# A hybrid layer on one core: one store for four normalisers, Silu in place of Sigmoid and multiply, and VectorE's work moved at five spots

## The chip, the cores and the metric

The kernel runs on one core of a Trainium2 chip, in one launch. The metric is the device time of one execution in microseconds (us). "Before" was run three times, and one more execution was profiled.

## The reference

One layer of a decoder trunk in float32, for 1024 prompt tokens and 8 samples of 8 tokens, which the kernel takes together as T = 1088 columns. `D_MODEL` is 1024 and `D_FF` 2816.

```python
h = rmsnorm(x, pre_mix_g)
proj = (h @ w_in).astype(f32)          # q, k, v, g of 4 retention heads; q, k, v, o of 4 mLSTM heads; 8 gate columns
gates = take(2 * N_ML_HEADS) + b_g
...
ret_y = head_groupnorm(ret_out, ret_g) * jax.nn.silu(g_r)
ml_out, C_new, n_new, m_new = mlstm_chunked(q_m, k_m * scale, v_m, i_pre, f_pre, C, n, m)
ml_y = head_groupnorm(ml_out, ml_g) * jax.nn.sigmoid(o_m)
...
mix = jnp.concatenate([ret_y, ml_y], axis=-1) @ w_out
x = x + rmsnorm(mix, post_mix_g)
h2 = rmsnorm(x, pre_ffn_g)
up = h2 @ w_up
...
conv = sum(padded[:, j:j + L] * conv_w[j] for j in range(CONV_W)) + conv_b
ffn = (jax.nn.gelu(gate, approximate=True) * val) @ w_down
x = x + rmsnorm(ffn, post_ffn_g)
```

Besides x it returns the heads' states, the mLSTM normalisers n and stabilisers m, and the last rows of the convolution's input. The normalisers of the samples, `n_sample`, are 4 heads x 8 samples x 128 numbers: the output `ns`.

## The kernel before

**Products.** Tokens lie along the free dimension, in four blocks of 272 columns. Every weight and every activation is split into a high and a low part (`split_to`: ScalarE copies the high part at L144, VectorE subtracts the low one at L146), and `product` (L160) makes three matmuls of 128x128 by 128x272 for each of 8 pieces of 128 rows: 24 matmuls for one block of 128 output columns. Names tell the weights: `in13` are columns 13 x 128 and on of `w_in`, and `in14_1` is block 1 of in14. A job of `proj` (L462) loads 512 KB of weights into one of two staging buffers (`stage_w`, SyncE's queue; tiles `st_...`), splits them (`wh_...`, `wl_...`), runs the four blocks, and hands each block's bank of PSUM to a function that empties it. The banks are two pools: `psA` with 2 banks, `psB` with 6.

**Stages.** 0 to 12 us start and loads; 12 to 60 q, k and v of the first retention head; 60 to 105 the eight gate columns and the swish gates in12 to in15; up to 500 the eight heads (`mix_head`, L537), the output gates in28 to in31 at the end; 500 to 602 the output projection; 602 to 650 the first up products, plain ones; 650 to 1075 the other up products, in a scheme of sums and differences of quadrants that saves products (`up_S`, `up_A`, L1101 to L1103), with the convolution (L1114, L1116) and the gelu; 1075 to 1307 the down products by the same scheme (`mm`, L1328 to L1330); then the last norm and the stores.

**What sets the order.** A scheduling layer places the instructions on each engine by its own estimate of when each can start; `tc.issue_after` pins one behind another. So the code's order is not the engines' order, and moved code may or may not move there. Tiles come from pools: `sb` has one buffer, a head's states, and the next head's load waits until all that reads it is done; the `sw` pool, from which the early gates take their tiles `z`, has two.

**The places that the change touches:**

- *A head's states.* `mix_head` loads `sb` at L593 (states) and L595 (normalisers, mLSTM only), `sample` (L699) updates it and stores it by `out_cs` (L732, 512 KB) and `out_ns` (L734, 128 x 8 numbers, each 4 bytes on its own). The next head's weights (`st_in..`) go through the same queue.
- *The swish gates.* `early_gate` (L504) reads a block's bank into `z` with VectorE (L509, times the token norm), ScalarE writes the sigmoid (L511), and VectorE multiplies it by `z` (L512). Meanwhile the generator `gate_rows` (L385) computes the mLSTM gates' cumulated logs on 4 rows of 1088 numbers, a step after each product (`next(rows)`).
- *The output gates.* `late_gate` (L515) does the same per block with a sigmoid, multiplied into `yT`. The last part of a head, its group norm (`finish`, L662: logs and exponentials), is put off into the next head's products by `held_back` and `finish_previous`; the last head's was not.
- *Between output and up projection.* `post_mix(b, t)` adds the residual; its `scale` (L962) computes a block's norm and the new operand. `combine` (L982) then forms four differences for each of two halves of the tokens, in place (L988, tiles `mo`), and `difference` (L1188) splits more of them, T2, T3 and T1, into operands. `prep` there is the preparation of the next up weights.
- *The down weights.* `prep_a` (L1268) loads quarters of a weight row (`wd`), and GpSimd forms their sums S3, S2, S1 and S4 in place (L1277, 44 instructions, 128x512). `halves` splits them and the activations (`rb`, `ra`) by ScalarE (L1255) and VectorE (L1256). VectorE also empties the down banks into `facc` (L1355).
- *The tail.* `norm_rows(0)` (L1397) sums squares for the first half of the tokens with six matmuls inside the last down product.

Of the kernel before, what the change touches and what calls it, by code (L numbers as in the profile page):

```python
# [16 lines left out]
P = 128  # L17
# [75 lines left out]
def hybrid_layer_kernel(ctx: ExitStack, tc: tile.TileContext, a: dict, o: dict):  # L93
# [410 lines left out]
    def early_gate(hid):  # L504
        def f(b, ps):
            o0, n = BLK[b]
            z = m2.tile([P, Q], F32, tag="sw", name=f"z_{hid}{b}")[:, :n]
            y = yT[hid // 2][:, hid % 2, o0:o0 + n]
            nc.vector.tensor_tensor(z, ps, rb[:, o0:o0 + n], ALU.mult)  # L509
            with tc.issue_after(last["rows"].ins):  # L510
                last["sigmoid"] = nc.scalar.activation(y, z, AF.Sigmoid)  # L511
            nc.vector.tensor_tensor(y, y, z, ALU.mult)  # L512
        return f

# [12 lines left out]

    EARLY = (0, 1, 2, 3)
    turns = {"wq": 0}
    early, held_back = [], []  # L530

    def finish_previous(b, row):

        if held_back:
            held_back.pop(0)(last["product", b], row)

    def mix_head(hd, ml):  # L537

        nm = ("m" if ml else "r") + str(hd)
        hid = hd + (NH if ml else 0)  # L540
        W = 129 if ml else P
        if hid == 0:
            vs = [tok(f"v_r{i}") for i in range(2)]
            proj(*((i, evac_copy(t), w) for i, t, w in zip(first, vs, wv)),
                 banks=lambda i, b: psB if b % 2 else psA, pair=True)
            early.extend(vs)
        v = early.pop(0) if early else tok(f"v_{nm}")
        q, k = tok(f"q_{nm}"), tok(f"k_{nm}")
        if ml:
            ub = ub_tile(f"ub{hd}")  # L550
            row = urows[hd:hd + 1, :]
            nc.sync.dma_start(ub, bass.AP(row.tensor, row.offset, [[0, P], [1, UB]]))
            proj((16 + hd, evac_norm(q, 1.0)))
            row = last["row", 3]
            proj((20 + hd, evac_norm(k, SCALE)), banks=lambda i, b: psB if b % 2 else psA)
            finish_previous(2, row)
            proj((24 + hd, evac_copy(v)))
            finish_previous(1, last["row", 3])
            finish_previous(2, last["row", 3])
        else:  # L560
            eq, ek = evac_rot(q, f"q{nm}"), evac_rot(k, f"k{nm}")
            if hd == 0:
                proj((0, eq, split_to(stage_w(a["wi"][0], "in0"), *first_q)), mid=pre_norm, banks=lambda i, b: psB)
                here["wq"] = mp.tile([P, 2, 2, 2 * P], F32, tag="wq", name="wq")
                proj((NH, ek))
            else:
                proj((hd, eq))
                row = last["row", 3]
                proj((NH + hd, ek))
                finish_previous(2, row)  # L570
                if hd == 1:
                    finish_previous(3, last["row", 1])
                    finish_previous(3, last["row", 2])
            if hd == 0:
                token_norms()
            if hd > 1:
                proj((2 * NH + hd, evac_copy(v)))
                finish_previous(1, last["row", 3])
                finish_previous(2, last["row", 3])
            if hd == 0:  # L580
                gate_proj()
                gate_consts()
                for _ in range(5):
                    next(rows)
                for i in range(NH):
                    proj((12 + i, early_gate(i)), banks=lambda i, b: psB if b % 2 else psA)
                    next(rows)
                    next(wsums)
                log_exp_tables(last["sigmoid"])
                next(rows)  # L590

        sb = m2.tile([P, NB, 129], F32, tag="sb", bufs=1, name=f"sb_{nm}")
        nc.sync.dma_start(sb[:, :, :P], a["sc" if ml else "sr"][hd].rearrange("p (s v) -> p s v", s=NB))  # L593
# [105 lines left out]
        def sample(kz, vt, qs, pt):  # L699
# [33 lines left out]
            if ml:  # L733
                nc.sync.dma_start(o["ns"][hd], sb[:, :, P])  # L734
            return lambda *order: finish(on, mv, 8, 1, f"{nm}s", *order)
# [37 lines left out]
        for i, cs in enumerate(order):  # L773
            cur, ready = ready, front(order[i + 1]) if i + 1 < len(order) else None
            done = sample(*cur) if cs == [8] else pair_of(cs[0], *cur)
            if todo and hid + 1 < 2 * NH:
                held_back.append(todo)
            elif todo:
                todo()
            todo = done  # L780
# [3 lines left out]
        nc.sync.dma_start(o["cp" if ml else "sp"][hd], S)  # L784
        if hid + 1 < 2 * NH:
            held_back.append(todo)
        else:
            todo()

# [63 lines left out]

    proj((28, late_gate(4)))
    proj((29, late_gate(5)))
    proj((30, late_gate(6)))
    w31 = split_to(stage_w(a["wi"][31], "in31"), mp.tile([P, D], F32R, tag="wq", name="w31_wq"), ub_tile("w31_ub", F32R)[:, :D])
    wo = [load_w(a["wo"][i], f"out{i}") for i in range(2)]
    order = last["split"]
    proj((31, late_gate(7), w31), done=lambda b: mix_split(b, order) if b < 2 else None)  # L860
    log_exp_tables(last["sigmoid"])
# [59 lines left out]
    def out_proj(b, steps=()):  # L921
# [17 lines left out]
        return [acc, *sq]  # L939

    def post_mix(b, t):

# [18 lines left out]

        def scale():  # L962
            nc.vector.tensor_tensor(xr[0][:, :2], xr[0][:, :2], xr[1][:, :2], ALU.add)  # L963
            last["xsum"] = nc.vector.tensor_tensor(xr[0][:, 0], xr[0][:, 0], xr[0][:, 1], ALU.add)
            rstd_block(xr[0][:, 0], t[1], t[2], t[0], f"pf{b}", last["product", 3] if b == 2 else last.get("fill"))
            for k in range(KT):
# [14 lines left out]

    def combine():  # L982
        q = [{(kh, th): mo[kh][th][:, :, qcols(i)] for kh in range(2) for th in range(2)} for i in range(2)]
        with tc.issue_after(last["scale"].ins):
            for o_, x, y in (((0, 0), (0, 1), (0, 0)), ((0, 1), (1, 1), (0, 1)),
                             ((1, 1), (1, 1), (0, 0)), ((1, 0), (1, 0), (1, 1))):
                for v in q:
                    nc.vector.tensor_tensor(v[o_], v[x], v[y], ALU.subtract)  # L988

# [11 lines left out]

    skip = lambda: None
    spaced = lambda f: [f[0], skip, f[1], f[2], skip, f[3]]
# [170 lines left out]
    plain(*firsts[1], 0)  # L1174
    scale()
    second_half(1)
# [8 lines left out]
    last["sq"], last["acc"] = last["split"]  # L1185
    combine()

# [5 lines left out]
    difference("T2", 4)  # L1193
    last["sq"], last["acc"] = last["split"]
    difference("T3", 6)
    last["sq"], last["acc"] = last["split"]
    difference("T1", 10)
    last["sq"], last["acc"] = last["split"]
    next(prep)
    cs_ = flat("c", 3, k=2)  # L1200
# [67 lines left out]
    def prep_a(q, p):  # L1268
# [5 lines left out]
        if q in sums_of:  # L1274
            out, x, y, op = sums_of[q]
            with tc.issue_after(last["S2"].ins) if q == 4 else nullcontext():
                last[out] = nc.gpsimd.tensor_tensor(quad(p, out), quad(p, x), quad(p, y), op)  # L1277
# [155 lines left out]
    for m in range(4):  # L1433
        for k in range(KH):
            mm(LAST, k, 1, m)
            if (m, k) == (1, 4):
                norm_rows(0)
                halves_of(3, (nc.gpsimd, nc.vector), quarter_0)
# [90 lines left out]
```

## Time and profile before

| | us |
|---|---|
| three runs | 1328.57, 1323.56, 1320.13 |
| their median | 1323.56 |
| profiled execution, its own time | 1321.61 |
| its span in the profile | 1319.7 |
| mean granted TensorE clock | 0.997 |
| outside the span | 1.9 |

The profile counts 10513 matmuls. It shows per engine the busy time (PE is TensorE's matmuls, PEld its weight loads, DVE VectorE, ACT ScalarE, POOL GpSimd, SP SyncE, whose work here is to issue transfers), groups of instructions by line, waits by what ended them, and a timeline. In a timeline's row the first number is the start, the second the duration, both us, and a bracket says how long the engine had been idle and what ended that. In a row of windows the figures behind the stretch are busy time and number of instructions of PE, PEld, DVE, ACT and POOL, then the granted clock, the DMA engines' share and GB/s. A row of the chain of waits has start, length, and the engine or transfer on which the end hung.

### The profile page before, as it was taken

How to read it: one execution, taken by the hardware profiler on the slowest of the kernel's cores; microseconds unless marked ns; L12 is line 12 of the kernel's file. 1: busy time of each engine (PE TensorE's matmuls, PEld its weight loads, DVE VectorE, ACT ScalarE, POOL GpSimd, SP SyncE). 2: the span in 40 equal slices, each digit the busy share in tenths (PEclk: the TensorE clock that was granted, in tenths of full speed). 3: DMA queues.
4: the chain of work that ended last, by engine and by line, in shares of the span. 5: the costliest groups of instructions: out<-in, count | busy, mean ns of one | idle time of the engine just before them, and what ended most of it. 6: DMA issues, size and time to landing. Idle time of an engine off the chain costs nothing.

```text
span 1319.7 us, 26829 instructions
## 1 busy us (share of the span) xinstructions
PE 1303.9 (99%) x10513; PEld 1289.4 (98%) x10513; DVE 1005.3 (76%) x2020; ACT 600.8 (46%) x1150; POOL 445.8 (34%) x564
## 2 busy tenths in 40 slices
PE   9999999999999999999999999999999999999996
PEld 9999999999999999999999999999999999999996
DVE  7777766657567666578999878787877888996678
ACT  7545433413423336445655434343433455454563
POOL 0353442757677100001445321222122214782002
PEclk9999999999999999999999999999999999999998
DMA  7334443558897224224044433444344369533363
GB/s 260 103 128 163 136 159 115 178 176 203 217 220 185 83 69 165 69 69 167 33 155 156 148 129 122 143 146 136 109 140 155 126 198 323 173 94 95 93 221 137
DMA packets 94416, 194.46 MB, mean 147 GB/s; under 512 B 17481, under 2 KB 42697, under 8 KB 93778
## 3 DMA queue, kind: packets, MB, share of 16 engines
q1 hardware_dynamic: 81986, 150.70, 34.6%
q0 software_dynamic: 12160, 41.95, 11.3%
q8 instruction: 82, 1.34, 0.4%
q14 instruction: 44, 0.36, 0.1%
q10 hardware_dynamic: 144, 0.11, 0.0%
HBM read 136.21 MB, written 56.50 MB: 146 GB/s over the span
## 4 chain that ended last, share of the span: by engine, by line
PE 86%; DVE 3%; DMA 2%; issue 1%; ACT 1%; SPq 0%; ACTq 0%; DVEq 0%
PE in L160 21%; PE out L160 7%; PE up_S L1103 6%; PE up_S L1101 6%; PE up_S L1102 6%; PE dn L1328 5%; PE dn L1329 5%; PE dn L1330 5%; PE up_A L1102 4%; PE up_A L1101 4%; PE up_A L1103 4%; DMA out_ns<-sb_m 2%; PE up_A L1153 1%; PE up_A L1152 1%; PE up_A L1151 1%; DVE facc L1405 1%
## 5 line engine op out<-in xcount | busy, mean ns | idle before, releaser
L160 PE MATMUL in<-hh,wh_in 128*128 128x272 f32 x960 | 278.8, 292 | 1.4 <-DVE z L509 1.3
L160 PE MATMUL in<-hl,wh_in 128*128 128x272 f32 x960 | 278.2, 292 | 0.0
L160 PE MATMUL in<-hh,wl_in 128*128 128x272 f32 x960 | 277.2, 291 | 0.0
L160 PEld LDWEIGHTS in<-hh,wh_in 128*128 128x128 f32 x960 | 180.4, 189 | 4.2 <-issue 3.1
L160 PEld LDWEIGHTS in<-hl,wh_in 128*128 128x128 f32 x960 | 180.0, 188 | 1.6 <-issue 1.3
L160 PEld LDWEIGHTS in<-hh,wl_in 128*128 128x128 f32 x960 | 180.5, 189 | 0.5 <-issue 0.3
L144 ACT ACTIVATE wh_up<-st_up 128x1024 fp32r<-128x1024 f32 x84 | 80.5, 959 | 163.6 <-PE up_S L1102 94.1
L146 DVE TENSOR_TENSOR wl_up<-st_up,wh_up 128x1024 fp32r<-128x1024 f32 x84 | 95.5, 1138 | 9.5 <-ACT wh_up L144 9.5
L1075 DVE TENSOR_TENSOR Uv<-Uv,up_S 128x272 f32<-128x272 f32 (+1 forms) x200 | 66.7, 377 | 46.6 <-PE up_S L1103 46.6
L1256 DVE TENSOR_TENSOR rb<-rb 128x544 fp32r<-128x544 f32 x78 | 77.1, 994 | 30.9 <-ACT rb L1255 29.3
L803 POOL TENSOR_TENSOR tab<-tab 128x256 f32<-128x256 f32 x104 | 84.5, 823 | 18.9 <-DMA tab<-in_wu 14.3
L1255 ACT ACTIVATE rb<-rb 128x544 fp32r<-128x544 f32 x78 | 50.5, 650 | 79.5 <-DMA rb<-bd 76.0
L1277 POOL TENSOR_TENSOR wd<-wd 128x512 f32<-128x512 f32 x44 | 73.2, 1683 | 39.7 <-DMA rb<-bd 13.0
L1136 POOL TENSOR_TENSOR act<-act 128x544 f32<-128x544 f32 x40 | 63.6, 1589 | 57.7 <-DMA bd<-act 35.4
L1116 DVE SCALAR_TENSOR_TENSOR c<-Uv,vec,c 128x1024 f32<-128x1024 f32 (+1 forms) x88 | 69.8, 799 | 8.6 <-ACT c L1114 8.6
L1116 DVE SCALAR_TENSOR_TENSOR c<-Ug,vec,c 128x1024 f32<-128x1024 f32 x88 | 67.8, 811 | 0.0
L1066 POOL MEMSET Ug<- 128x2 f32 x22 | 2.2, 99 | 193.3 <-DVE xr L963 80.9
L803 POOL TENSOR_TENSOR wq<-wq 128x256 f32<-128x256 f32 x56 | 48.6, 878 | 46.6 <-DMA wq<-in_wu 44.4
L144 ACT ACTIVATE wh_in<-st_in 128x1024 fp32r<-128x1024 f32 (+2 forms) x31 | 31.9, 1028 | 55.0 <-PE in L160 48.4
L1114 ACT ACTIVATE c<-Ug,vec 128x1024 f32<-128x1024 f32 (+1 forms) x44 | 34.6, 833 | 44.3 <-DVE Ug L1079 42.4
L803 POOL DMA_DIRECT2D tab<-in_wu x52 | 36.8, 713 | 50.2 <-DVE k_r L499 23.6
L146 DVE TENSOR_TENSOR wl_in<-st_in,wh_in 128x1024 fp32r<-128x1024 f32 (+2 forms) x31 | 39.2, 1263 | 13.1 <-ACT wh_in L144 12.9
(554 smaller groups left out, 4688.5 us busy)
## 6 DMA issues: line engine op xcount, KB each, us to landing
rb<-bd SPq DMA_DIRECT2D x76, 272.0 KB, 3.0
st_up<-sd SPq DMA_DIRECT2D x40, 512.0 KB, 3.7
bd<-act SPq DMA_DIRECT2D x33, 544.0 KB, 4.5
st_in<-in_wi SPq DMA_DIRECT2D x31, 512.0 KB, 4.3
tab<-in_wu POOLq DMA_DIRECT2D x52, 256.0 KB, 5.3
sd<-tab POOLq DMA_DIRECT2D x26, 512.0 KB, 4.1
st_up<-in_wu SPq DMA_DIRECT2D x24, 512.0 KB, 3.3
wd<-in_wd SPq DMA_DIRECT2D x44, 256.0 KB, 4.6
```

What stands on the lines that cost most here:

```text
L144: act = nc.scalar.activation(hi, x, AF.Copy)
L146: last["split"] = act, eng.tensor_tensor(lo, x, hi.bitcast(F32), ALU.subtract)
L160: last["product", b] = nc.tensor.matmul(ps, u[:, k * P:(k + 1) * P], x[b // 2][k // 4][v][:, k % 4, qcols(b)], start=k == term == 0, stop= ...
L803: last["sums"] = f(*args)
L1075: nc.vector.tensor_tensor(o_, o_ if x is None else c(x), c(ps), ALU.add)
L1101: nc.tensor.matmul(ps, wh[:, c], xh[:, k, n], start=k == 0, stop=False)
L1102: nc.tensor.matmul(ps, wh[:, c], xl[:, k, n], start=False, stop=False)
L1103: nc.tensor.matmul(ps, wl[:, c], xh[:, k, n], start=False, stop=k == 3)
L1116: last["conv"] = nc.vector.scalar_tensor_tensor(c, u(i), cw(i), c, ALU.mult, ALU.add)
L1256: nc.vector.tensor_tensor(lo, x, hi.bitcast(F32), ALU.subtract)
L1277: last[out] = nc.gpsimd.tensor_tensor(quad(p, out), quad(p, x), quad(p, y), op)
L1328: nc.tensor.matmul(t, wh[:, ms], ah, start=k == 0, stop=False)
```

## The change

It does eight things:

1. The samples' normalisers are copied by VectorE from `sb` into one tile `norms`, a copy of 128x8 for each head, and stored once, after the last head, in pieces of 32 bytes. The four stores of 4-byte pieces go.
2. The staging load of the next mLSTM head's first weights (`staged`) is written ahead of the load of `sb`.
3. The swish gates use Silu, so that VectorE's 16 multiplies (L512) go.
4. The output gates in28 and in29 keep their sums in a whole row `z`, and one sigmoid and one multiply of 128x1088 follow for each; the last head's group norm is put off into them, so that its logs come ahead of the sigmoids. Products of in28 to in31, and k of the retention heads, take banks of both pools in turn.
5. `combine` is cut into its halves, and the first half's four differences are allowed into `scale`'s gaps.
6. The next up weights are prepared ahead of T3 and T1.
7. GpSimd's S4 sums are pinned behind the last S1 of all rows.
8. `norm_rows(0)` comes two steps later in the last down product.

```diff
@@ early_gate, gate_row
-                last["sigmoid"] = nc.scalar.activation(y, z, AF.Sigmoid)
+                last["sigmoid"] = nc.scalar.activation(y, z, AF.Silu)
+        return f
+
+    def gate_row(hid):
+        z = tok(f"z_{hid}")
+        def f(b, ps):
+            o0, n = BLK[b]
+            nc.vector.tensor_tensor(z[:, o0:o0 + n], ps, rb[:, o0:o0 + n], ALU.mult)
+        def apply():
+            y = yT[hid // 2][:, hid % 2]
+            with tc.issue_after(last["exp"].ins):
+                last["sigmoid"] = nc.scalar.activation(z, z, AF.Sigmoid)
             nc.vector.tensor_tensor(y, y, z, ALU.mult)
-        return f
+        return f, apply
@@ mix_head
-            proj((16 + hd, evac_norm(q, 1.0)))
+            proj((16 + hd, evac_norm(q, 1.0), split_w(staged.pop(), f"in{16 + hd}")))
...
+        if hid >= NH - 1:
+            j = 12 + hid + 1 if hid + 1 < 2 * NH else 28
+            staged.append(stage_w(a["wi"][j], f"in{j}"))
         sb = m2.tile([P, NB, 129], F32, tag="sb", bufs=1, name=f"sb_{nm}")
...
             if ml:
-                nc.sync.dma_start(o["ns"][hd], sb[:, :, P])
+                nc.vector.tensor_copy(norms[:, hd], sb[:, :, P])
+                if hd == NH - 1:
+                    nc.sync.dma_start(o["ns"].rearrange("h p s -> p h s"), norms)
...
-        if hid + 1 < 2 * NH:
-            held_back.append(todo)
-        else:
-            todo()
+        held_back.append(todo)
@@ the output gates
-    proj((28, late_gate(4)))
-    proj((29, late_gate(5)))
-    proj((30, late_gate(6)))
+    gates_mid = [gate_row(hid) for hid in (4, 5)]
+    proj((28, gates_mid[0][0], split_w(staged.pop(), "in28")), banks=alternate)
+    finish_previous(3, None)
+    proj((29, gates_mid[1][0]), banks=alternate)
+    finish_previous(1, None)
+    finish_previous(2, None)
+    for _, apply in gates_mid:
+        apply()
+    proj((30, late_gate(6)), banks=alternate)
@@ scale, combine
-        def scale():
+        def scale(between=skip):
...
+            between()
             rstd_block(xr[0][:, 0], t[1], t[2], t[0], ...)
...
-    scale()
+    scale(lambda: combine(0, last["xsum"]))
...
-    combine()
+    combine(1, last["scale"])
...
     difference("T2", 4)
+    next(prep)
     difference("T3", 6)
     difference("T1", 10)
-    next(prep)
@@ prep_a
-            with tc.issue_after(last["S2"].ins) if q == 4 else nullcontext():
+            with tc.issue_after(last[SEQ[q - 1][0] if q == 5 else "S2"].ins) if q > 3 else nullcontext():
@@ the last down product
-            if (m, k) == (1, 4):
+            if (m, k) == (1, 6):
                 norm_rows(0)
```

What stands in the engines' order at three places. First SyncE's queue in the mLSTM heads, around the end of head m1 and the start of m2 (`ub` is a table for the head, `out_cp` the prompt's state). Before:

```order
L132 DMA st_in19_5433<-in_wi 128x1024
L784 DMA out_cp<-S_m17_4704 128x129
L552 DMA ub3_5431<-urows_250 128x1160
L732 DMA out_cs<-sb_m1_4510 1024x1x128
L734 DMA out_ns<-sb_m1_4510 1024x1x1
L593 DMA sb_m2_5177<-in_sc 128x8x128
L595 DMA sb_m2_5177<-in_sn 128x8x1
L132 DMA st_in23_5543<-in_wi 128x1024
```

After:

```order
L132 DMA st_in19_5162<-in_wi 128x1024
L804 DMA out_cp<-S_m17_4691 128x129
L569 DMA ub3_5418<-urows_250 128x1160
L752 DMA out_cs<-sb_m1_4497 1024x1x128
L613 DMA sb_m2_5164<-in_sc 128x8x128
L615 DMA sb_m2_5164<-in_sn 128x8x1
L132 DMA st_in23_5528<-in_wi 128x1024
```

Only the store of the normalisers is gone; the first weights of the head after (st_in19) already stood ahead of the load of `sb_m2` before.

Second, VectorE in the gate stage, from the z of in13's block 2 to that of in14's block 2. The rows with 4x1088 are the generator's, `wl_in15` is the low part of weights. Before:

```order
L509 TENSOR_TENSOR z_12_1067<-in13_2_1042,rb_84 128x272
L509 TENSOR_TENSOR z_13_1096<-in13_3_1071,rb_84 128x272
L146 TENSOR_TENSOR wl_in15_1245<-st_in15_1242,wh_in15_1244 128x1024
L422 TENSOR_TENSOR yT3_819<-yT3_819,small_252 4x8
L512 TENSOR_TENSOR yT0_816<-yT0_816,z_12_1067 128x272
L512 TENSOR_TENSOR yT0_816<-yT0_816,z_13_1096 128x272
L425 SCALAR_TENSOR_TENSOR yT3_819<-yT3_819 4x1088
L509 TENSOR_TENSOR z_20_1139<-in14_0_1114,rb_84 128x272
L509 TENSOR_TENSOR z_21_1168<-in14_1_1143,rb_84 128x272
L428 COPY small_252<-yT3_819 4x8 x2
```

After:

```order
L509 TENSOR_TENSOR z_12_1062<-in13_2_1037,rb_84 128x272
L417 TENSOR_TENSOR yT2_819<-yT3_820,yT2_819 4x1088
L423 MEMSET yT3_820 4x8
L509 TENSOR_TENSOR z_13_1090<-in13_3_1065,rb_84 128x272
L146 TENSOR_TENSOR wl_in15_1234<-st_in15_1231,wh_in15_1233 128x1024
L422 TENSOR_TENSOR yT3_820<-yT3_820,small_252 4x8
L509 TENSOR_TENSOR z_20_1132<-in14_0_1107,rb_84 128x272
L425 SCALAR_TENSOR_TENSOR yT3_820<-yT3_820 4x1088
L428 COPY small_252<-yT3_820 4x8 x2
L432 TENSOR_TENSOR yT2_819<-yT2_819,yT3_820 4x1088
L429 COPY small_252<-small_252 4x7
L509 TENSOR_TENSOR z_21_1160<-in14_1_1135,rb_84 128x272
```

The multiplies of L512 are gone, and the z of in14's block 0 now stands ahead of the scan L425.

Third, GpSimd in the down stage, where the sums S2 of the eleven weight rows end and the next begin (one tile `wd` per row). Before:

```order
L1277 TENSOR_TENSOR wd_13446<-wd_13446 128x512
L1277 TENSOR_TENSOR wd_13447<-wd_13447 128x512
L1277 TENSOR_TENSOR wd_13437<-wd_13437 128x512 x2
L1277 TENSOR_TENSOR wd_13438<-wd_13438 128x512 x2
L1277 TENSOR_TENSOR wd_13439<-wd_13439 128x512 x2
L1277 TENSOR_TENSOR wd_13440<-wd_13440 128x512 x2
```

After:

```order
L1301 TENSOR_TENSOR wd_13420<-wd_13420 128x512
L1301 TENSOR_TENSOR wd_13421<-wd_13421 128x512
L1301 TENSOR_TENSOR wd_13411<-wd_13411 128x512
L1301 TENSOR_TENSOR wd_13412<-wd_13412 128x512
L1301 TENSOR_TENSOR wd_13413<-wd_13413 128x512
L1301 TENSOR_TENSOR wd_13414<-wd_13414 128x512
```

Before, a row's S2 and S4 stood together; now all S2 come first, then all S1, then all S4.

More of the change, by code (lines that the diff above doesn't have):

```diff
@@ L528, in hybrid_layer_kernel @@
     EARLY = (0, 1, 2, 3)
+    alternate = lambda i, b: psB if b % 2 else psA
     turns = {"wq": 0}
-    early, held_back = [], []
+    early, held_back, staged = [], [], []
     def finish_previous(b, row):
@@ L535, in finish_previous @@
             held_back.pop(0)(last["product", b], row)
+    norms = mp.tile([P, NH, NB], F32, name="norms")
     def mix_head(hd, ml):
@@ L544, in mix_head @@
             proj(*((i, evac_copy(t), w) for i, t, w in zip(first, vs, wv)),
-                 banks=lambda i, b: psB if b % 2 else psA, pair=True)
+                 banks=alternate, pair=True)
             early.extend(vs)
@@ L552, in mix_head @@
             nc.sync.dma_start(ub, bass.AP(row.tensor, row.offset, [[0, P], [1, UB]]))
-            proj((16 + hd, evac_norm(q, 1.0)))
+            proj((16 + hd, evac_norm(q, 1.0), split_w(staged.pop(), f"in{16 + hd}")))
             row = last["row", 3]
-            proj((20 + hd, evac_norm(k, SCALE)), banks=lambda i, b: psB if b % 2 else psA)
+            proj((20 + hd, evac_norm(k, SCALE)), banks=alternate)
             finish_previous(2, row)
@@ L568, in mix_head @@
                 row = last["row", 3]
-                proj((NH + hd, ek))
+                proj((NH + hd, ek), banks=alternate)
                 finish_previous(2, row)
@@ L585, in mix_head @@
                 for i in range(NH):
-                    proj((12 + i, early_gate(i)), banks=lambda i, b: psB if b % 2 else psA)
+                    proj((12 + i, early_gate(i)), banks=alternate)
                     next(rows)
@@ L775, in mix_head @@
             done = sample(*cur) if cs == [8] else pair_of(cs[0], *cur)
-            if todo and hid + 1 < 2 * NH:
+            if todo:
                 held_back.append(todo)
-            elif todo:
-                todo()
             todo = done
@@ L784, in mix_head @@
         nc.sync.dma_start(o["cp" if ml else "sp"][hd], S)
-        if hid + 1 < 2 * NH:
-            held_back.append(todo)
-        else:
-            todo()
+        held_back.append(todo)
     sd = dr.tile([JT, P, 4, D // 2], F32, name="sd")
@@ L859, in hybrid_layer_kernel @@
     order = last["split"]
-    proj((31, late_gate(7), w31), done=lambda b: mix_split(b, order) if b < 2 else None)
+    proj((31, late_gate(7), w31), banks=alternate, done=lambda b: mix_split(b, order) if b < 2 else None)
     log_exp_tables(last["sigmoid"])
@@ L939, in out_proj @@
         return [acc, *sq]
+    skip = lambda: None
     def post_mix(b, t):
@@ L980, in operands, with combine @@
         X[name] = [slot(s0 + i, f"{name}{'hl'[i]}") for i in range(2)]
[L982 to L988, printed above, removed]
+    def combine(i, after):
+        q = {(kh, th): mo[kh][th][:, :, qcols(i)] for kh in range(2) for th in range(2)}
+        for o_, x, y in (((0, 0), (0, 1), (0, 0)), ((0, 1), (1, 1), (0, 1)),
+                         ((1, 1), (1, 1), (0, 0)), ((1, 0), (1, 0), (1, 1))):
+            with tc.issue_after(after.ins):
+                nc.vector.tensor_tensor(q[o_], q[x], q[y], ALU.subtract)
     def first_half(i, after=None):
@@ L1000, in second_half @@
             split(name, i, mo[kh][1][:, :, qcols(i)])
-    skip = lambda: None
     spaced = lambda f: [f[0], skip, f[1], f[2], skip, f[3]]
```

## The prediction

> **What bounds the kernel now.** I read the busy times first, then the slices of TensorE, then its waits, then the timeline around each wait. The page's busy line and TensorE's row of slices:
>
> ```profile
> PE 1303.9 (99%) x10513; PEld 1289.4 (98%) x10513; DVE 1005.3 (76%) x2020; ACT 600.8 (46%) x1150; POOL 445.8 (34%) x564
> ...
> PE   9999999999999999999999999999999999999996
> ```
>
> TensorE is the bound, and only the last slice shows a gap. A busy TensorE need not be at its best pace, so the next thing is the price of one matmul. From the windows, a long stretch of up products, then the start and the end of the span:
>
> ```profile
> 720.00:1100.00 380.00, 380.00 (x3034) 380.00 (x3033) 307.09 (x546) 162.84 (x212) 93.37 (x170) 1.00 0.44 148
> 0.00:12.00 12.00, 10.80 (x66) 10.07 (x67) 5.62 (x14) 7.69 (x14) 0.71 (x9) 1.00 0.82 289
> 1307.00:1319.70 12.70, 1.46 (x7) 0.60 (x5) 9.04 (x11) 2.30 (x5) 1.34 (x1) 0.72 0.39 155
> ```
>
> 380 us for 3034 matmuls are 125 ns for each, at the full granted clock (1.00). The change has exactly as many matmuls as before, of the same shapes, so what it can win is only the time in which TensorE waits. Outside the first 12 and the last 12.7 us, which the change leaves as they are, I look for starts of neighbouring matmuls that lie further apart than 125 ns. The list of TensorE's waits (total, count, longest in us):
>
> ```profile
> PE in L160 <- DVE z L509: 1.3, 2, 1.1
> PE u_m L750 <- ACT vts L623: 1.0, 1, 1.0
> PE up_S L1101 <- ACT Uv L1086: 0.7, 1, 0.7
> PE dn L1328 <- DVE facc L1355: 0.4, 1, 0.4
> ```
>
> and TensorE's timeline on both sides of the longest of each kind:
>
> ```profile
> 99.02 0.29 PE L160 MATMUL in<-hl,wh_in 128*128 128x272 f32 x1
> 100.41 0.36 PE L160 MATMUL in<-hh,wh_in 128*128 128x272 f32 x1 [1.10 <-DVE z L509]
> ...
> 349.00 0.28 PE L160 MATMUL in<-hh,wl_in 128*128 128x272 f32 x1
> 350.29 0.38 PE L750 MATMUL u_m<-vts,kz_m 128*128 128x129 f32 x1 [1.00 <-ACT vts L623]
> ...
> 680.00 0.28 PE L1103 MATMUL up_S<-T2h,wl_up 128*128 128x272 f32 x1
> 680.94 0.40 PE L1101 MATMUL up_S<-B3h,wh_up 128*128 128x272 f32 x1 [0.66 <-ACT Uv L1086]
> ...
> 1142.86 0.29 PE L1330 MATMUL dn<-rb,ra_dlo 128*128 128x272 f32 x1
> 1143.57 0.39 PE L1328 MATMUL dn<-rb,ra_dhi 128*128 128x272 f32 x1 [0.42 <-DVE facc L1355]
> ```
>
> Starts apart, less 0.125 for the slot that a matmul needs anyway: (a) 1.39 gives 1.26 us in the swish gates, and the list's second wait there 1.3 - 1.1 = 0.2, together 1.5; (b) 1.29 gives 1.16 in head m1; (c) 0.94 gives 0.81 in the first up sums; (d) 0.71 gives 0.58 in the down products. Together 1.5 + 1.2 + 0.8 + 0.6 = 4.1 us, 0.3% of the span. That is the whole stake of the change; all else is whether it opens new waits.
>
> **Swish gates (parts 3 and 4).** VectorE at the long wait of (a), with two of the multiplies that Silu makes needless (L512):
>
> ```profile
> 95.18 1.87 DVE L512 TENSOR_TENSOR yT<-yT,z 128x272 f32<-128x272 f32 x2
> 97.08 2.84 DVE L425 TENSOR_TENSOR_SCAN yT<-yT 4x1088 f32<-4x1088 f32 x1
> 99.86 0.75 DVE L509 TENSOR_TENSOR z<-in,rb 128x272 f32<-128x272 f32 x2
> ```
>
> TensorE wants the bank that the z at 99.86 empties; VectorE is ready to empty it only then, because it first does two multiplies (1.87) and the scan (2.84). In the new order the multiplies are gone and the scan stands behind that z. So it comes about 1.87 + 2.84 = 4.7 us earlier, at about 95.2, against 99.02 when TensorE needs the bank: 3.8 us in hand. The short wait has the same cause, multiplies ahead of its z. I take the whole 1.5. The trace of before shows no Silu. I price it like the Sigmoid it replaces, one instruction on the same 128x272; the bounds are a gain of 1.5 and, if z is held up again elsewhere, a loss worked out as the last rival.
>
> The other half of this edit gathers eight sigmoids and eight multiplies of the output gates into two and two, and lets the last head's logs go first. TensorE has no gap there:
>
> ```profile
> 360.00:500.00 140.00, 140.00 (x1167) 137.06 (x1166) 94.05 (x297) 51.37 (x141) 55.88 (x69) 1.00 0.53 138
> ```
>
> TensorE is busy 140.00 of 140 us, and VectorE idles 46 us of it, so fewer instructions on VectorE and ScalarE buy nothing: 0. The cover is the products in28 to in31 themselves; more bank room (both pools in turn) can only loosen it.
>
> **Normalisers and weights (parts 1 and 2).** The chain of waits that leads into (b), and from the page the median time to landing of the states' own store:
>
> ```profile
> 318.16 20.82 DMA out_ns<-sb_m
> 339.06 0.60 SPq L593
> ...
> 340.97 6.94 DMA st_in<-in_wi
> 347.94 1.06 ACT wh_in L144
> ...
> 350.29 0.75 PE u_m L750 x4
> ...
> out_cs<-sb_m SPq DMA_DIRECT2D x4, 512.0 KB, 9.3
> ```
>
> The store of 1024 pieces holds `sb` for 20.82 us. The next states' load must wait for it, at the head of SyncE's queue, and the weights behind that load (st_in, 6.94) reach ScalarE only at 347.94, just when ScalarE should prepare `vts` for TensorE: it does the split first (1.06), and TensorE is 1.16 late. With the change the load waits for `out_cs` instead, issued just ahead of `out_ns`, and for a copy of 128x8. At 9.3 us to landing the load goes at about 318 + 9.3 + a fraction = 328 and not at 339.06, and the split comes 11 us earlier, near 337, under products that run without a gap. I take 1.16. The other end: ScalarE's split now meets another small step of the head and makes that late by at most its own length, 1.06, a net gain of 0.1. What the change adds is four copies on VectorE, which is busy 94.05 of 140 us in the row above, and one store at the end, for which nothing waits. On SyncE's queue weights of the output projection stand behind it; but it needs no more than `out_cs` ahead of it, a last update of `sb`, so it holds them up by the length of an issue, 0.60 as at 339.06, against the 20.82 that went: 0.
>
> The weights written ahead of the states' load: in the order of SyncE's queue they already stood ahead, so 0, and this part doesn't do what it says.
>
> **Sums and differences (parts 5 and 6).** From VectorE's timeline the residual, the differences and T1, then TensorE's first use of T1, and ScalarE's instruction behind (c):
>
> ```profile
> 628.45 0.44 DVE L212 TENSOR_SCALAR oacc<-ssqb_pf 128x272 f32<-128x272 f32 x1 [3.19 <-ACT oacc L211]
> ...
> 638.45 6.10 DVE L988 TENSOR_TENSOR mo<-mo,mo 128x1088 f32<-128x1088 f32 x5
> ...
> 651.60 2.50 DVE L146 TENSOR_TENSOR T1l<-mo,T1h 128x1088 fp32r<-128x1088 f32 x2
> 654.00 1.23 DVE L146 TENSOR_TENSOR wl_up<-st_up,wh_up 128x1024 fp32r<-128x1024 f32 x1
> 655.28 1.48 DVE L1116 SCALAR_TENSOR_TENSOR c<-Ug,vec,c 128x1024 f32<-128x1024 f32 x2
> ...
> 657.85 0.29 PE L1101 MATMUL up_S<-T1h,wh_up 128*128 128x272 f32 x1
> ...
> 680.49 0.69 ACT L1086 ACTIVATE Uv<-up_A 128x272 f32<-128x272 f32 x2 [3.20 <-DVE c L1116]
> ```
>
> VectorE's backlog is what ends (c): ScalarE waits 3.20 for the convolution there. One difference costs 6.10 / 5 = 1.22 us; three of the first half's four now stand in the gap of 3.19. They fill it whole, and the last overhangs by 3 x 1.22 - 3.19 = 0.5. So VectorE gets 3.2 us of otherwise idle time, of which at worst 0.5 is lost twice (the scale ends later, and what waits for it): 2.7 to 3.2, more than the 0.81 of (c). T1 now stands behind the next weights' subtraction (1.23) and three passes of the convolution (0.74 each): with no gain at all its low part would end at 654.1 + 1.2 + 2.2 = 657.5, still ahead of TensorE's first use of T1 at 657.85. So 0 for that, and 0.8 for (c). The ends: 0.8, and -0.5 if VectorE's list behind the moved work simply closes up, the convolution stays last and the overhang is paid.
>
> **Down products (part 7).** Splits of `rb` on VectorE without and beside GpSimd, GpSimd's sums, and VectorE's spare time later:
>
> ```profile
> 1122.56 0.72 DVE L1256 TENSOR_TENSOR rb<-rb 128x544 fp32r<-128x544 f32 x1
> 1128.34 1.81 DVE L1256 TENSOR_TENSOR rb<-rb 128x544 fp32r<-128x544 f32 x1
> ...
> 1122.72 20.15 POOL L1277 TENSOR_TENSOR wd<-wd 128x512 f32<-128x512 f32 x12 [6.88 <-DVE ra_dhi L1256]
> ...
> 1160.00:1180.00 20.00, 20.00 (x162) 20.00 (x161) 20.00 (x14) 9.96 (x22) 19.46 (x12) 1.00 0.27 82
> 1180.00:1200.00 20.00, 20.00 (x162) 20.00 (x162) 16.46 (x22) 8.33 (x15) 4.59 (x3) 1.00 0.40 112
> 1200.00:1220.00 20.00, 20.00 (x163) 20.00 (x162) 13.21 (x22) 8.49 (x14) 7.27 (x8) 1.00 0.30 88
> ```
>
> The same split takes 0.72 alone and 1.81 beside GpSimd's sums: 1.09 more. From 1122.72 on GpSimd runs 12 sums in one piece, S2 and S4 in pairs, and at its end, near 1142.9, VectorE empties a bank too late for TensorE: (d). With S4 pinned behind all S1, about half of the 12 leave this stretch. Six splits at 1.09 less are 6.5 us of backlog, against 0.58: I take 0.6. The eleven S4 sums come back after the last S1, near 1185 by GpSimd's busy time (19.46 of 20 up to 1180), where VectorE has 20 - 16.46 + 20 - 13.21 = 10.3 us to spare. Eleven at 1.09 cost 12.0. The difference of 1.7 us is the worst there; since not each sum meets a split, I take 0.
>
> [...]
>
> **Part 8**: six matmuls, two steps later in a product without a gap: 0.
>
> **The sum.** 1.5 + 1.2 + 0.8 + 0.6 = 4.1 us off. The profiled execution took 1321.61 (its span 1319.7 and 1.9 around it), 2 us under the median of 1323.56. One execution against three: I start from the middle of both, 1322.6. 1322.6 - 4.1 = 1318.5.
>
> **The rivals.**
>
> 1. *The waits on VectorE only move.* VectorE is the busiest engine after TensorE in both stages: in the up sums (c) a backlog returns once T1 and the weights are split, and in the down stage the S4 sums meet VectorE with 1.7 too little. For it speaks the row 1160 to 1180, full to 20.00; against it that VectorE has 10 us just behind. (a) and (b) are won, 2.7; (c) is not, and (d) becomes 0.6 - 1.7, a loss of 1.1: 1322.6 - 2.7 + 1.1 = 1321.0.
> 2. *Nothing of it is seen.* The three runs of before scatter over 8.4 us, twice the stake, and the gaps may be filled by other small waits (a TensorE that comes 1.5 us earlier to the heads finds their loads 1.5 us less early). The time is then 1322.6, up to 1328.
> 3. *Slower: the ring of two tiles z.* A tile z is now freed by ScalarE's Silu and not by VectorE's multiply. VectorE may not write block n+2's z until Silu n is done, and ScalarE does its queue in order, weight splits of 1.06 among it (the row at 347.94). If each of the 14 blocks behind the first two came as late as the one at 100.41 (1.26), that were 17.6 us; with (b), (c), (d) won and (a) lost, 1322.6 - 2.6 + 17.6 - 1.5 = 1336, slower by just 1%. It decides when a Silu comes later than two blocks after its product, 2 x 24 x 0.125 = 6.0 us. A split of 1.06 in front of it is a sixth of that, and before, the multiply too waited for ScalarE's sigmoid in the same queue. So this needs a queue six splits long.
>
> **How the numbers follow.** 0.6 for the four gaps closed or nearly (1318.5), 0.2 for the first rival (1321.0), 0.15 for the second (1322.6 to 1328), 0.03 for the third (1336). 0.02 is left for faster by more than I can account for: over 1% would need 13 us, and only the start and the end hold so much. The range's low end is the fastest run of before less the whole stake and 2 us for a luckier draw, 1320.1 - 4.1 - 2 = 1314; its high end is the slowest run shown with nothing won, 1328. Within 1%, 13 us, is about what a measurement of this kernel can tell from no change; by the same cases faster by more is 0.02, within 0.94, slower by more 0.04 (the third rival and a hundredth for what I didn't see).
>
> **What would show it.** (a): no wait of TensorE on z between 85 and 105 us, and the z of in14's block 0 ahead of the scan. (b): no `out_ns` in the chain; the states' load some 10 us after `out_cs`; no wait on vts. (c): none on Uv near 681. (d): single splits near 0.8 in 1122 to 1143, no wait on facc there, nor a new one in 1175 to 1205 (the first rival). Wrong would be the whole account if TensorE showed a wait of over 2 us between 12 and 1307 that before did not have, or if the end behind the last dense product grew from 12.7 us.

## The result

| | us | runs |
|---|---|---|
| before, median (range) | 1326.3 (1320.1 to 1328.6) | 6 |
| after, median (range) | 1316.22 (1315.82 to 1317.02) | 6 |
| after, profiled execution, its own time | 1316.31 | 1 |
| its span | 1314.4 (before: 1319.7) | 1 |

The ratio is 0.9932, with a 95% interval of 0.9911 to 0.9953: faster by 0.7%, within the 1% for which the prediction gave 0.94. Two things stand in the table. The spans of the two profiled executions differ by 5.3 us, which is near the forecast of 4.1; the medians differ by 10. And the times of before spread over 8.4 us, those of after over 1.2. So the change took away something that the one profiled execution of before shows only in part.

The profile after, first the page's busy times and chain of waits by engine:

```profile
PE 1301.4 (99%) x10513; PEld 1289.1 (98%) x10513; DVE 996.8 (76%) x2002; ACT 600.1 (46%) x1144; POOL 435.1 (33%) x564
...
PE 96%; DVE 2%; DMA 1%; ACT 1%; issue 0%; SPq 0%
```

TensorE's matmuls are as many as before, and its share of the chain rose from 86% to 96%. TensorE's waits in full (total, count, longest, us):

```profile
PE ssqb_fin L210 <- ACT facc_sq L1364: 1.3, 1, 1.3
PE warm L155 <- DVE ones L200: 1.1, 1, 1.1
PE in L160 <- ACT wh_in L144: 0.3, 1, 0.3
```

The four kinds of wait that the prediction priced are gone; what is left lies in the first 12 us and in the tail. From SyncE's timeline, the store of a head's states and the load of the next, in head m1 before, then in m1 and m3 after:

```profile
317.52 0.59 SPq L732 DMA_DIRECT2D out_cs<-sb_m  x1
339.06 0.60 SPq L593 DMA_DIRECT2D sb_m<-in_sc  x1
...
314.86 0.59 SPq L752 DMA_DIRECT2D out_cs<-sb_m  x1
324.12 0.55 SPq L613 DMA_DIRECT2D sb_m<-in_sc  x1
...
412.08 0.59 SPq L752 DMA_DIRECT2D out_cs<-sb_m  x1
415.75 0.55 SPq L613 DMA_DIRECT2D sb_m<-in_sc  x1
```

The load follows the store by 9.3 and 3.7 us, where before it came 21.5 us behind `out_cs`. In the up sums, VectorE now does the differences (L1013) while it would have waited for the norm:

```profile
620.92 3.94 DVE L1013 TENSOR_TENSOR mo<-mo,mo 128x1088 f32<-128x1088 f32 x3
624.81 0.44 DVE L212 TENSOR_SCALAR oacc<-ssqb_pf 128x272 f32<-128x272 f32 x1
```

In the down stage, splits on VectorE in the stretch that was disturbed, GpSimd's sums, VectorE around the end of these sums, and the windows there:

```profile
1123.52 0.72 DVE L1280 TENSOR_TENSOR rb<-rb 128x544 fp32r<-128x544 f32 x1 [0.57 <-ACT rb L1279]
1124.16 1.78 DVE L1280 TENSOR_TENSOR ra_wlo<-wd,ra_wlo 128x512 fp32r<-128x512 f32 x1
1126.94 0.73 DVE L1280 TENSOR_TENSOR rb<-rb 128x544 fp32r<-128x544 f32 x1 [1.00 <-ACT rb L1279]
...
1149.26 39.52 POOL L1301 TENSOR_TENSOR wd<-wd 128x512 f32<-128x512 f32 x23 [0.63 <-DVE ra_whi L1280]
...
1185.85 1.78 DVE L1280 TENSOR_TENSOR ra_wlo<-wd,ra_wlo 128x512 fp32r<-128x512 f32 x1
1187.56 1.81 DVE L1280 TENSOR_TENSOR rb<-rb 128x544 fp32r<-128x544 f32 x1
1189.29 0.68 DVE L1280 TENSOR_TENSOR ra_dhi<-wd,ra_dhi 128x512 fp32r<-128x512 f32 x1
1189.89 0.71 DVE L1280 TENSOR_TENSOR rb<-rb 128x544 fp32r<-128x544 f32 x1
...
1180.00:1200.00 20.00, 20.00 (x162) 20.00 (x161) 18.62 (x23) 7.71 (x13) 11.41 (x9) 1.00 0.31 84
```

In the disturbed stretch the splits of `rb` mostly take 0.73 again and leave VectorE idle between them; the splits of weights (`ra`) next to them still meet one of the S2 sums and take 1.78. The sums of S1 and S4, 22 of the 23 in the row, follow in one piece up to 1188.8. As long as that piece runs, the splits take about 1.8 us each, and right behind it 0.68 and 0.71. VectorE was busy 18.62 of 20 us in 1180 to 1200 (16.46 before, when the same work came about 5 us later), and TensorE lost nothing.

The prediction named one sign that did come up, though it is small: the stretch behind the start of the last down matmul grew from 12.8 to 13.1 us (the prediction counts 12.7 from 1307.00). The table behind the experiments takes it up.

### The profile page after: what moved, and what is told of

Read it like the earlier page. It is cut to its first block, busy times and chain, and to the rows that moved or that the text cites. A ratio compares the mean times of both kernels' runs of the same rounds, so it can differ in the third digit from the quotient of the medians.

```text
span 1314.4 us, 26808 instructions
## 1 busy us (share of the span) xinstructions
PE 1301.4 (99%) x10513; PEld 1289.1 (98%) x10513; DVE 996.8 (76%) x2002; ACT 600.1 (46%) x1144; POOL 435.1 (33%) x564
## 4 chain that ended last, share of the span: by engine, by line
PE 96%; DVE 2%; DMA 1%; ACT 1%; issue 0%; SPq 0%
PE in L160 29%; PE out L160 7%; PE up_S L1127 6%; PE up_S L1126 6%; PE up_S L1125 6%; PE dn L1352 5%; PE dn L1353 5%; PE dn L1354 5%; PE up_A L1126 5%; PE up_A L1125 5%; PE up_A L1127 5%; PE up_A L1177 1%; PE up_A L1176 1%; PE up_A L1175 1%; DVE facc L1429 1%; PE s_r L665 1%
## 5 line engine op out<-in xcount | busy, mean ns | idle before, releaser
L820 POOL TENSOR_TENSOR tab<-tab 128x256 f32<-128x256 f32 x104 | 80.8, 787 | 12.2 <-DMA tab<-in_wu 7.8
```

Source lines behind the costliest of these rows:

```text
L820: last["sums"] = f(*args)
```

## The experiments

Each kernel was timed beside runs of before on the same chip. Medians of before on the three chips were 1326.13, 1324.21 and 1323.05, so the kernels are compared by their own medians and ranges, by the waits in their profiles, and at the end by the lengths of the stages in them. Two theories were to be told apart. One: the four stores of the normalisers take a different time in each execution, and this is both the larger gain and the spread. The other: the spread comes from VectorE's backlog in the later stages.

**Before, once more**

> The kernel before, unchanged, for a second profile and more times. The six times of before spread over 8.4 us (1320.1 to 1328.6), those of the changed kernel over 1.2 us. Theory (normalisers' stores): the 4-byte stores take a different time in each execution, so this profile shows out_ns at other lengths than 20.8, 16.2 and 13.0 us and the waits of TensorE on vts and on weights in the heads m1 to m3 change with it, by several us; the gates (1.5), the up sums (0.8) and the down products (0.6) wait as before. Rival (VectorE's backlog): the heads lose 1.2 as before and the spread shows in the gates, the up sums or the down products.

1327.16 (1320.0 to 1330.32, 12 runs). Its profiled execution took 1322.75, again one of the shorter ones: the waits were 0.6 on vts, 0.7 on z, 0.7 on Uv, 0.4 on facc, and 0.3 in a later head. So the heads' waits do change from one execution to the next, in this list by tenths; the wait on z changes too (1.3 before). The list leaves out short waits: from the first matmul of head m0's states (`u_m`) to the first of the sums `up_S`, TensorE took 358.79 us here and 357.19 in the first profile, 1.6 us more, while the gate stage was 0.6 us shorter. That speaks for the first theory, but two profiles are few.

**Before with the normalisers' part alone**

```diff
-                nc.sync.dma_start(o["ns"][hd], sb[:, :, P])
+                nc.vector.tensor_copy(norms[:, hd], sb[:, :, P])
+                if hd == NH - 1:
+                    nc.sync.dma_start(o["ns"].rearrange("h p s -> p h s"), norms)
```

> The kernel before with the normalisers' part alone: four copies into a tile and one store. Theory: no wait of TensorE in the heads m1 to m3, and most of the 10 us goes: about 1319 (1316.2 plus the 2.9 of the three other waits), with times that spread over some 2 us. Rival: 1.2 us is won, 1325, and the spread stays at 8 us.

1319.98 (1318.96 to 1321.42, 11 runs): 6.1 us under the median of before on this chip, and the spread falls from 11 us to 2.5. The heads show no wait. This is near the theory's 1319; the rival's 1325 is outside the range. SyncE's timeline has the load 7.0 us behind the store in head m1:

```profile
316.20 0.59 SPq L734 DMA_DIRECT2D out_cs<-sb_m  x1
323.24 0.55 SPq L595 DMA_DIRECT2D sb_m<-in_sc  x1
```

**After with the four stores put back**

```diff
-                nc.vector.tensor_copy(norms[:, hd], sb[:, :, P])
-                if hd == NH - 1:
-                    nc.sync.dma_start(o["ns"].rearrange("h p s -> p h s"), norms)
+                nc.sync.dma_start(o["ns"][hd], sb[:, :, P])
```

> The changed kernel with the normalisers' four stores put back. Theory: the wait in the heads comes back, 1317.4 in a lucky execution and 5 us and more above 1316.2 in others, with the spread of before. Rival: 1317.4, with a spread of 1 to 2 us.

1321.7 (1315.94 to 1331.35, 12 runs). The spread is back, 15 us wide, and the median is 5.5 us up on the 1316.22 of the result. The shortest run is as short as the changed kernel's: the stores cost nothing in an execution in which they land early. The profile caught one of the short ones, 1316.85: the stores took 15.5 and 15.9 us and TensorE waited for nothing in the heads.

**Before with Silu alone**

```diff
-                last["sigmoid"] = nc.scalar.activation(y, z, AF.Sigmoid)
-            nc.vector.tensor_tensor(y, y, z, ALU.mult)
+                last["sigmoid"] = nc.scalar.activation(y, z, AF.Silu)
```

> The kernel before with Silu in the swish gates alone. Theory of the prediction: the two waits of TensorE on z near 93 and 100 us go, 1.5 us; nothing else moves, so the time is 1.5 us below before and spreads as before. Rival (ring of two tiles): a new wait on z in the gate stage, no gain or a loss.

1325.09 (1318.68 to 1333.96, 12 runs), ratio 0.9989 with an interval of 0.9967 to 1.0012: a gain of 1 us can't be told in this spread. But the profile has no wait on z, and it caught the longest of the twelve executions, which is worth more. Its SyncE timeline:

```profile
315.23 0.59 SPq L731 DMA_DIRECT2D out_cs<-sb_m  x1
315.88 0.76 SPq L733 DMA_DIRECT2D out_ns<-sb_m  x1
340.40 0.60 SPq L592 DMA_DIRECT2D sb_m<-in_sc  x1
...
373.65 0.67 SPq L733 DMA_DIRECT2D out_ns<-sb_m  x1
396.37 0.60 SPq L592 DMA_DIRECT2D sb_m<-in_sc  x1
```

its first wait on TensorE's timeline:

```profile
347.01 0.28 PE L160 MATMUL in<-hh,wl_in 128*128 128x272 f32 x1
352.84 0.80 PE L749 MATMUL u_m<-vts,kz_m 128*128 128x129 f32 x2 [5.55 <-ACT vts L622]
```

and the windows around it (the granted clock is the third figure from the end):

```profile
340.00:347.00 7.00, 7.00 (x60) 7.00 (x59) 0.42 (x1) 0.40 (x1) 5.21 (x9) 1.00 0.75 232
347.00:353.00 6.00, 0.45 (x4) 0.23 (x2) 1.42 (x1) 2.50 (x6) 5.53 (x8) 0.92 0.98 353
353.00:356.00 3.00, 3.00 (x14) 3.00 (x15) 2.22 (x7) 1.84 (x7) 2.73 (x5) 0.50 0.82 208
356.00:360.00 4.00, 4.00 (x25) 4.00 (x25) 2.72 (x9) 2.04 (x7) 3.62 (x6) 0.64 0.81 301
360.00:364.00 4.00, 4.00 (x37) 4.00 (x36) 3.75 (x17) 2.76 (x9) 3.30 (x6) 1.00 0.67 220
```

The store holds `sb` for 24.5 us instead of 20.8, and TensorE waits 5.55 us instead of 1.00, because the slack that hides the first 19 to 20 us (24.5 - 5.55, 20.8 - 1.0) is used up. Then the wait costs a second time: the clock granted behind it is 0.50 and 0.64 for about 7 us. The windows give the price: 39 matmuls in 353 to 360, where the pace behind it (37 in 4 us) would make 65, so about 2.8 us are lost behind the wait of 5.55 (an estimate). Two such waits (5.55 and 3.88, 9.4 us in the list) put this execution's span at 1331.9, 14.9 us above the 1317.0 of the kernel with the normalisers' part and Silu below. So the wait and the clock together cost about 1.6 times the wait here (14.9 / 9.4).

Behind the wait of 5.55 (353 to 356), behind the one of 3.88 (409 to 412) and behind one of 4.9 in the next kernel (356 to 360) the granted clock was 0.50. Behind the wait of 1.00 in before it was not: it stayed at 1.00 (346 to 370).

**Copies, but still four stores of 4-byte pieces**

```diff
-                nc.sync.dma_start(o["ns"][hd], sb[:, :, P])
+                nc.vector.tensor_copy(norms[:, hd, :, 0], sb[:, :, P])
+                nc.sync.dma_start(o["ns"][hd], norms[:, hd, :, 0])
```

(`norms` has two places for each number here, so that the pieces stay at 4 bytes.)

> The kernel before with a copy of each head's normalisers into a tile of its own, from which the same four stores of 4-byte pieces go. Theory (the store holds the one buffer of sb, and with it the queue): the stores take as long as before, but the states' load no longer waits for them; no wait on vts in the heads, time and spread like those of the kernel with the normalisers' part alone, 1320 and 2.5 us. Rival (the 4-byte pieces slow the weights' transfers on the way): the waits stay, 1324 to 1326 with a spread of 8 us or more.

1321.27 (1319.55 to 1328.65, 12 runs), between the two; against before on the same chip the ratio is 0.9982, with an interval of 0.9963 to 1.0002. Its profile caught the longest of the twelve. SyncE's timeline, then TensorE's longest wait:

```profile
316.86 0.59 SPq L734 DMA_DIRECT2D out_cs<-sb_m  x1
317.50 0.67 SPq L737 DMA_DIRECT2D out_ns<-norms  x1
335.65 0.60 SPq L595 DMA_DIRECT2D sb_m<-in_sc  x1
```

```profile
PE u_m L753 <- ACT vts L625: 4.9, 1, 4.9
```

Nothing waits for `out_ns` any more, but `out_cs` itself, issued 0.6 us ahead of it, now lets the load go only 18.8 us later, against 7.0 with one store at the end. In the two heads behind it the load comes 14.5 and 12.7 us after `out_cs`, against 9.7 and 3.7. So the theory was half right, and so was its rival: the store holds the one buffer, and its pieces also delay the store that runs beside them.

**Copies, and four stores of 32-byte pieces** (as the last one, with `norms[:, hd]` in one piece)

> The kernel before with a copy of each head's normalisers, and a store for each head from that tile, in pieces of 32 bytes. Theory (both the hold of sb and the 4-byte pieces on the way cost): with both gone it is as good as one store at the end: about 1320, no wait on vts, spread about 2.5 us, the states' load 4 to 10 us behind out_cs. Rival (a store in the middle of the heads costs by itself): waits and a spread as in the kernel with copies and 4-byte pieces, 1321 to 1328.

1319.4 (1318.94 to 1320.94, 12 runs), as good as one store at the end. The load goes 9.8, 9.1 and 3.6 us behind `out_cs`, and there is no wait on vts. This kernel and the last one differ only in the size of the pieces and in the layout of `norms` that makes it, so it isn't the number of stores that matters but the size of the pieces and the hold. Why the 4-byte stores take longer in one execution than in another, no run shows.

**Three parts, each on top of the normalisers' part.** Silu as above; the differences with the earlier preparation (parts 5 and 6); and the S4 pin (part 7), whose one line is

```diff
-            with tc.issue_after(last["S2"].ins) if q == 4 else nullcontext():
+            with tc.issue_after(last[SEQ[q - 1][0] if q == 5 else "S2"].ins) if q > 3 else nullcontext():
```

> The kernel before with the normalisers' part and Silu. Prediction: up to 1.5 us below the normalisers' part alone (1319.98), 1318.5, and no wait on z in the profile. Rival: the profile of the normalisers' part alone showed no wait on z either, so the wait is one of some executions only, and the gain is 0 to 1 us.

> The kernel before with the normalisers' part, the first half of the differences in the gaps of the residual, and the next weights ahead of T3 and T1. Prediction: the wait on Uv near 680 goes, 0.8 us: 1319.2. Rival: the wait stays or comes back later in the up sums, 1320.

> The kernel before with the normalisers' part and GpSimd's S4 sums behind all S1. Prediction: the wait on facc near 1141 goes, 0.5 us: 1319.4. Rival (the wait moves to where the S4 sums now meet VectorE): a wait between 1175 and 1205, 1320 to 1321.7.

Against 1319.98 for the normalisers' part alone (2.5 us of spread): Silu 1318.88 (1318.12 to 1320.43), no wait on z. Differences 1319.04 (1318.22 to 1320.46), no wait on Uv. S4 pin 1319.13 (1318.12 to 1321.38), no wait on facc and none in 1175 to 1205. The gains of 1.1, 0.9 and 0.85 all rest on the one 1319.98, which is from another chip; against the 1319.4 of the kernel with 32-byte pieces, from a third, they would be 0.5, 0.4 and 0.3. So these times show no more than a gain of some tenths each. That the waits on Uv and on facc go with their parts, the profiles show. The wait on z was absent from the normalisers' part alone too: it is there in five of the seven profiles with Sigmoid and the multiply (0.4 to 1.3 us) and in none of the seven with Silu.

**Two parts taken back from the changed kernel**, beside the changed kernel on one chip.

> The changed kernel again, beside the next three on one chip: 1316.2, spread 1 to 2 us. No wait of TensorE above 0.3 us between 12 and 1300 us.

1316.25 (1316.13 to 1317.68, 6 runs). Before took 1323.05 on this chip (18 runs), so the whole change is worth 6.8 us here, and 10 in the runs of the result: how much before loses to its stores differs between sets of runs.

> The changed kernel with the output gates and the last head's end as before (a sigmoid and a multiply for each block, no banks in turn, k of the retention heads in its old banks). Prediction: this part is worth 0, so 1316.2 as the changed kernel. Rival: the parts measured one by one leave about 0.9 us unexplained (1319.98 less 1.1, 0.9 and 0.9 is 1317.1, against 1316.2); if it is here, 1317.1.

The edit restores `late_gate` for in28 and in29, the last head's end and the old banks, as in the diff of the change. 1316.72 (1316.43 to 1317.84, 6 runs): 0.5 us, with no wait of TensorE between 12 and 1300 us in the profile. The table below shows where it is: 0.3 between the first retention head and the first mLSTM head, where the edit changes only the banks of k, and 0.2 behind that.

> The changed kernel with GpSimd's S4 sums where they were. Prediction: the wait on facc comes back near 1139, 0.6 us: 1316.8 to 1317.1. Rival: with the other parts in place VectorE has caught up by then, no wait, 1316.2.

1317.07 (1316.76 to 1317.96, 7 runs): 0.8 us, and its list of waits has one entry more than the changed kernel's in the down stage:

```profile
PE dn L1352 <- DVE facc L1379: 0.4, 1, 0.4
```

**Parts 2 and 8** took no run of their own. For part 2 there are the timelines: with the normalisers' part alone and with the whole change, SyncE issues the same transfers in the same order from 260 to 450 us, as far as the names in the rows tell, so the weights stand where they stood. Part 8 is argued below.

**The stages of all profiles.** Starts of matmuls cut TensorE's work into stretches that hold the same number of matmuls in every kernel: up to the first `u_r` (the first retention head's states), to the first `u_m`, to the first `up_S`, to the first `dn`, to the last `dn`, and to the end. Their lengths in us do not depend on comparing chips by medians:

| profile | to `u_r` | to `u_m` | to `up_S` | to `dn` | to last `dn` | to the end |
|---|---|---|---|---|---|---|
| before | 119.37 | 180.78 | 357.19 | 416.35 | 233.30 | 12.8 |
| normalisers' part | 118.11 | 180.70 | 355.95 | 416.38 | 233.17 | 12.9 |
| and Silu | 117.92 | 180.52 | 355.95 | 416.00 | 233.65 | 12.9 |
| and differences | 117.86 | 180.88 | 355.93 | 415.22 | 233.53 | 12.9 |
| and S4 pin | 118.74 | 180.52 | 355.95 | 416.62 | 232.51 | 12.9 |
| after without part 4 | 117.62 | 180.53 | 355.96 | 415.21 | 232.32 | 13.1 |
| after without S4 pin | 117.72 | 180.23 | 355.78 | 415.21 | 233.10 | 13.0 |
| after | 117.69 | 180.23 | 355.78 | 415.21 | 232.32 | 13.1 |

The normalisers' part, the differences, the S4 pin and part 4 each show in a column of their own; Silu belongs in the first, which scatters from execution to execution. The third column also settles where the spread comes from: it is 357.19, 358.79, 364.05 and 371.15 in the four profiles of kernels with 4-byte stores on the base of before, where each of the other columns stays within 1.8 us.

## Why the prediction was right, and where it was off

The forecast was 1318.5 within 1314 to 1328; measured were 1316.2. That the time came out within 2.3 us is in part luck: the start of the sum, 1322.6, was 3.7 us below the median of the six runs of before, and the gain of 4.1 was 6 us short of the 10 measured; the two errors offset each other. By its own steps:

- *TensorE is the bound, and only its waits can be won*: right. All four waits went, and no new one of more than 0.3 us came between 12 and 1307 us. Between the two profiles the last down matmul starts 5.8 us earlier, where the four waits were put at 4.1; by the columns of the table the gains are 1.7, 1.4, 1.1 and 1.0 where the waits of 1.5, 1.2, 0.8 and 0.6 were read, and 0.6 in the retention heads, where none was. 0.5 of it all is part 4, which had been put at 0; for the rest, short waits that the list leaves out are likely but were not counted.
- *(a) Swish gates, 1.5*: about 0.9. The mechanism holds (z ahead of the scan, multiplies gone): the first `u_r` starts at 117.6 to 117.9 us in the seven profiles with Silu and at 117.9 to 119.4 in the seven without, 0.9 apart in the mean. The mis-sized step is "it first does two multiplies (1.87) and the scan (2.84)", which are the lengths of one execution. In the kernel with the normalisers' part alone the same rows are shorter. GpSimd's sums beside them, in that kernel's profile and then in the first profile of before, show why:

```profile
90.02 5.30 POOL L807 TENSOR_TENSOR wq<-wq 128x256 f32<-128x256 f32 x4 [2.84 <-DMA wq<-in_wu]
95.45 0.79 DVE L512 TENSOR_TENSOR yT<-yT,z 128x272 f32<-128x272 f32 x2
96.27 2.41 DVE L425 TENSOR_TENSOR_SCAN yT<-yT 4x1088 f32<-4x1088 f32 x1
...
94.07 3.58 POOL L803 TENSOR_TENSOR wq<-wq 128x256 f32<-128x256 f32 x4 [4.46 <-DMA wq<-in_wu]
```

Where the sums end ahead of the multiplies (at 95.3), the pair takes 0.79; where they run beside them (up to 97.7), it takes 1.87. So it is in all seven profiles with the multiplies: 1.87 to 1.89 in five, 0.79 in the two in which the sums had ended. When the sums begin depends on a load of weights.
- *(b) Normalisers, 1.2*: the wait was rightly traced to the store that holds `sb`, and its size was wrong by a factor of three to five. The step that was mis-sized is "TensorE is 1.16 late", taken as what the store costs. Measured were 6.1 us on before and 5.5 on after, and 3.7 on the third chip (1323.05 against 1319.4 with 32-byte pieces). The wait is what is left of some 20 us once the slack is used up, so 4 us more of landing made it 5.7 instead of 1.2; and behind the waits of 3.88 us and more the granted clock was 0.50. What the prediction didn't have at all is that the 4-byte pieces also delay `out_cs` (the load 18.8 us behind it, against 9.8 with 32-byte pieces): with the hold alone removed, part of the loss stayed (1321.27 against 1319.4).
- *(c) Differences, 0.8, and (d) S4 sums, 0.6*: 1.2 by the stretch to `dn` (416.38 against 415.22), and 0.7 to 0.8 by the stretch behind it and by the run without the pin, with the waits gone where they were said to go. In (d), "single splits near 0.8" holds for those of `rb`; about every second split still meets a sum and takes 1.78.
- *Weights ahead of the states' load, 0*: right, by the order. *The output gates, 0*: 0.5 measured for part 4, of which 0.3 lies at the banks of k.
- *Part 8, 0*: the end behind the last down matmul grew, which the prediction had named as a sign that its whole account is wrong. It is 12.7 to 12.9 us in the nine profiles on the base of before and 13.0 to 13.1 in the five on the base of after. As a sign it was set too sharply: it says nothing of the four waits. Part 8 is the change nearest to it, but it was not tried alone.

The rivals: that the waits only move (1321.0) fell. The S4 sums did meet VectorE where it was said, and slowed its splits there, but TensorE did not wait. The splits took 1.78 and 1.81 us beside the sums in the new place, as 1.81 in the old, and 0.68 and 0.71 behind them. The prediction's reason for taking 0 there, "since not each sum meets a split", did not hold: VectorE went from split to split without a pause until the sums ended (busy 39.40 of 39.40 us from 1149.3 to 1188.7). TensorE had its operands in time even so. That nothing of it is seen (1322.6 and up) fell in the most useful way: the scatter of before, which that rival counted as noise, was not noise of the measurement but the stores' own work, and went with them. The ring of two tiles z did not hold anything up: no profile with Silu shows a wait on z.

## What to carry to other kernels

A spread of times that is much wider than a wait in the profile is itself a finding: one profiled execution can be among the shortest, and a wait that is only the visible end of a long hidden transfer should be priced by how that transfer's length varies, not by the one wait. Write small outputs that lie scattered in a big buffer into a tile of their own and store that, in longer pieces: here, in head m1, the next load into the buffer went 7.0 us behind the states' store and not 21.5, and with a store in each head 9.8 us behind it with pieces of 32 bytes, 18.8 with pieces of 4. Ask of each wait of TensorE whether the clock falls behind it (here it did behind waits of 3.88 us and more), since two such waits of 9.4 us in all cost 14.9 here, about 1.6 times their length. And compare the starts of the same matmul in several profiles: where executions scatter by more than the parts are worth, the lengths of the stages still tell the parts apart.

## What the runs showed of the hardware

- 1024 pieces of 4 bytes, 4 KB in all, landed 7.9 us (by the load that waited for them) to 28.5 us after their issue. Stored from a tile of their own, they delayed the 512 KB store issued ahead of them: the load behind that store went 18.8, 14.5 and 12.7 us after it in the three heads, against 9.8, 9.1 and 3.6 with pieces of 32 bytes.
- After waits of 3.88, 4.9 and 5.55 us the granted clock was 0.50 for about 3 us and more, where one of 1.0 us left it at 1.00; nothing in between was measured.
- VectorE's split of `rb` (128x544) took mostly 1.8 us (1.43 to 1.82) where GpSimd's sums ran on without a pause, and 0.71 to 0.73 where none ran or the split began just ahead of one; in the gate stage two multiplies of 128x272 took 1.87 beside GpSimd's sums and 0.79 behind them.
